# Second layer of an encoder: token rows of x through DRAM in 32x32 blocks instead of TensorE transposes

## The chip, the cores and the metric

The kernel runs on one core of a Trainium2 chip. The metric is the device time in microseconds of one execution. A core has TensorE (PE, matrix products into PSUM), VectorE (DVE), ScalarE (ACT), GpSimd (POOL) and SyncE (SP, which here only issues transfers). Transfers are carried out by 16 DMA engines that all queues share; SP, ACT and POOL issue them, and each of these queues works in its own order.

## What is computed

A two-layer encoder over 512 tokens of width 1024, in fp32: a stick-breaking attention block and an MLP, then a gated linear recurrence block and an MLP, then a last normalisation. The part that matters is the second MLP and what follows:

```
h = rms_norm(x, norm_mlp[1])
u = relu(h @ w1);  x = x + (u * u) @ w2
out = rms_norm(x, norm_final)
```

Every product is made of three fp32r products (high half times high half, low times high, high times low), so each operand is first split: ACT casts the high half (`wh`), DVE subtracts it to get the low half (`wl`).

## The kernel before

x lies with features on partitions: eight tiles `x[c]` of 128 features x 512 tokens. The MLP's hidden layer is computed in four quarters of 1024 features. The first quarter's hidden units come from `squared(c)`, c = 0 to 7 (24 matmuls each). What follows are 98 steps of 24 matmuls (2.72 us each): a "down" stage of 14 steps (indices 0 to 13) for the first quarter, then for each of three quarters an "up" stage and a "down" stage of 14 steps. In down stages the result has tokens on partitions; `y(t, h)` is the half-row h (512 features) of the token block t (128 tokens), one half of a tile c0 to c3. Products are formed by a seven-product scheme (P1 to P7), so weight blocks (`b11`, `b12`, `b22`, `b21`) are added to each other first: by DVE, or, for P7 and P4 and one P6, by a transfer on POOL that adds in place (`added`, L1096; "add" below). The result of an add is cast and split (`operand`) four steps before PE uses it.

`collect` (L1119) takes a finished product out of PSUM into `y`: where the tile is in `begun`, DVE scales it and adds it to what is there (L1125); else ACT writes it scaled (L1128) and puts it into `begun`.

Since the result must be x plus the MLP, the second layer puts x itself into `y` first. `between(c)` (L1659) is called behind each `squared(c)`; for c = 0 to 3 it transposes token block c of all eight chunks on PE into two PSUM banks, ACT copies the banks to `y` (L1670), and all eight half-rows are marked as begun. Behind c = 3, 4 and 5, `sums_of_x` (L924) overwrites x in place, chunk by chunk.

The chunks 7 of two tiles, `bh` and `bl`, hold something else early in the first down stage and are moved away by `replace` (L988, on ACT) in the steps 5, 7, 10 and 11.

The order on PE is that of the program. ACT's and DVE's steps inside the MLP are chained in program order (`Ordered`, L772). POOL's and SP's instructions are put in order at build time by a scheduler that lets ready ones pass others. The program is built with `dynamic_dma_scratch_size=1024` (L1833), the scratch for POOL's transfers. In `run`, `load(i)` (L1217) comes first in each step, then `leave(i-1)` with the collects and operands.

Of the kernel before, what the change touches and what calls it, by code (L numbers as in the profile page):

```python
# [2 lines left out]

# [8 lines left out]
F32 = mybir.dt.float32  # L12
F32R = mybir.dt.float32r
AF = mybir.ActivationFunctionType
ALU = mybir.AluOpType
PSUM = bass.MemoryType.PSUM

P = 128
S = 512
D = 1024  # L20
C = D // P
# [6 lines left out]
ASIDE, FRONT = 16, 64  # L28


START = [
# [31 lines left out]
def hybrid_encoder(  # L63
# [23 lines left out]
    nc = tc.nc  # L87
# [16 lines left out]
    def f(ap):  # L104
        return ap.bitcast(F32)
# [36 lines left out]
    bh = const.tile([P, C, S], F32R, tag="bh", name="bh")  # L142
# [164 lines left out]
    def home_tile(tag, n, name):  # L307
        return home.tile([P, S], F32, tag=tag, name=name, bufs=n)
# [482 lines left out]
    class Mlp:  # L791
# [28 lines left out]
        def __init__(self, ctx, layer):  # L820
            self.layer, self.sq, self.first = layer, Squares(), None
            self.V, self.A = Ordered(V), Ordered(A)
            self.mp = ctx.enter_context(tc.tile_pool(name=f"mlp{layer}", bufs=2))
            self.c = [
                self.mp.tile([P, 2, S], F32, tag=f"c{i}", name=f"c{i}", bufs=1) for i in range(4)
            ]
            self.begun, self.a = set(), {}
            self.turns = count(4 * layer)
            self.blocks = ExitStack()
            self.bp = self.blocks.enter_context(tc.tile_pool(name=f"blocks{layer}", bufs=2))  # L830
            self.u, self.lows, self.s3, self.slots = {}, {}, {}, None

            t = self.bp.tile([P, C // 2 * S + ASIDE], F32R, tag="s41", name="s41", bufs=1)
            self.s41 = t[:, : C // 2 * S].rearrange("p (k s) -> p k s", s=S)
# [316 lines left out]
        def run(self, first, between, end):  # L1151
# [13 lines left out]
            def place(i):  # L1165

                return (i + self.STEPS // 2) % self.STEPS
# [48 lines left out]

            def load(i):  # L1217
                q4, at = steps[i][1], place(i)

                if i == 0:  # L1220
                    self.turns = count(2)
                elif at == 0:
                    self.turns = count(4)
                    self.u.clear()
                    del self.a[1]
                elif at == 4:
                    units["down", q4] = self.from_down(q4)
                    self.load(units["down", q4], (0, "b11"), (0, "b12"), (1, "b11"))
                elif at == 11:
                    self.load(units["down", q4], (1, "b12"), (0, "b22"), (1, "b22"))  # L1230
                elif at == 14 and q4 == NQ - 1:
                    end.ready()
                elif at == 22 and q4 < NQ - 1:
                    units["up", q4 + 1] = self.from_up(q4 + 1)
                    self.load(units["up", q4 + 1], (0, "b11"), (0, "b12"), (0, "b22"), (1, "b11"))
                elif at == 25 and q4 < NQ - 1:
                    self.load(units["up", q4 + 1], (1, "b12"), (1, "b22"))
# [145 lines left out]
    with ExitStack() as mctx:  # L1383
# [29 lines left out]
        def between(c):  # L1413
            for n in {0: (0, 4), 1: (1, 5), 2: (2, 6), 3: (3,), 4: (7,)}.get(c, ()):
                nc.sync.dma_start(out=away[:, n, :], in_=x[n])
            if c == C - 1:
                soft.send(mlp.ready)
# [31 lines left out]
    with ExitStack() as rctx:  # L1449
# [44 lines left out]
        def fetch(key):  # L1494
            i = int(key[1:]) + (C if key[0] == "c" else 0)
            pool = wmore if next(fetched) % 4 == 3 else wpool
            raws[key] = pool.tile([P, C, P], F32, tag="raw", name="raw", bufs=3 if pool is wpool else 1)
            nc.sync.dma_start(out=raws[key], in_=w_ro[i] if key[0] == "o" else w_in[i])
# [157 lines left out]
    with ExitStack() as mctx:  # L1656
        mlp = Mlp(mctx, 1)

        def between(c):  # L1659

            t = c
            if t not in range(NB):
                return
            for h in range(2):
                pt = mlp.bank()
                for i in range(4):
                    PE.transpose(
                        pt[:, i * P : (i + 1) * P], x[4 * h + i][:, t * P : (t + 1) * P], ident
                    )
                A.copy(mlp.y(t, h), pt)  # L1670
                mlp.begun.add((t // 2 * 2 + h, t % 2))

        gb = []

        def factors():
            for h in range(2):
                gb.append(home_tile(*HOMES[h], "gb"))
                nc.sync.dma_start(
                    out=gb[h], in_=g_final[:, h * S : (h + 1) * S].broadcast_to([P, S])
                )  # L1680


        A.activation(mlp.c[0][:, 0, :1], eps_t, AF.Sqrt)

        free = colt[:, COLS["conv"][0] :]
        ss = free[:, : 3 * NB].rearrange("p (t i) -> p t i", i=3)
        bias = free[:, 3 * NB : 4 * NB]

        EV, EA = Ordered(V), Ordered(A)

        def square(t, h, i, cols=slice(0, S), end=False):

            junk = work.tile([P, S], F32, tag="sq", name="junk")
            EA.activation(
                junk[:, cols], mlp.y(t, h)[:, cols], AF.Square, accum_out=ss[:, t, i : i + 1]
            )
            if not end:
                EA.activation(
                    bias[:, t : t + 1], ss[:, t, i : i + 1], AF.Identity,
                    bias=bias[:, t : t + 1] if i else eps_t, scale=1.0 / D,  # L1700
                )

        def scaled(t, h, cols=slice(0, S), e=G):
            y = mlp.y(t, h)[:, cols]
            e.tensor_tensor(y, y, gb[h][:, cols], ALU.mult)

        def root(t, i):

            rt = work.tile([P, 1], F32, tag="rt", name="rt")
            EA.activation(rt, ss[:, t, i : i + 1], AF.Sqrt, bias=bias[:, t : t + 1], scale=1.0 / D)  # L1710
            EV.reciprocal(rt, rt)
            return rt

        def leaves(t, h, queue):
            queue.dma_start(out=out[t * P : (t + 1) * P, h * S : (h + 1) * S], in_=mlp.y(t, h))

        def scaled_half(t, h, rt, queue):

            y = mlp.y(t, h)
            EA.activation(y, y, AF.Copy, scale=rt)  # L1720
            leaves(t, h, queue)

        def whole_half(t, h, rt, cut=None, last=None):

            y = mlp.y(t, h)
            with tc.issue_after(last.ins) if last else nullcontext():
                EV.scalar_tensor_tensor(
                    y[:, cut:], y[:, cut:], rt, gb[h][:, cut:],
                    ALU.mult, ALU.mult,
                )  # L1730
            if cut:
                EV.tensor_scalar(y[:, :cut], y[:, :cut], rt, None, ALU.mult)
            leaves(t, h, nc.sync)

        def end(ws, xs):
            for t in range(2):
                square(t, 0, 0)
                scaled(t, 0)
                square(t, 1, 1, end=True)
                rt = root(t, 1)  # L1740
                scaled_half(t, 0, rt, nc.sync)
                whole_half(t, 1, rt, last=mlp.gained)
            for t in range(2, 4):
                square(t, 1, 0)
            scaled(2, 1)
            for g in range(2):
                mlp.times("P4", g, 0, ws[g], xs[0], False)
            mlp.collect("P4", 1, xs[1])
            for e in (EV, EA):
                e.turn(True)  # L1750
            mlp.V = EV
            mlp.collect("P4", 0, xs[0])
            square(2, 0, 1, end=True)
            halves = [slice(i * HS, (i + 1) * HS) for i in range(2)]
            ps = [mlp.bank()[:, :HS] for _ in halves]
            for i, cols in enumerate(halves):
                for g in range(2):
                    mlp.times("P4", g, 1, ws[g], ps[i], True, cols)
            mlp.collect("P4", 1, ps[0], halves[0])
            rt = root(2, 1)  # L1760
            square(3, 0, 1, halves[0])
            scaled_half(2, 1, rt, nc.sync)
            whole_half(2, 0, rt)
            mlp.collect("P4", 1, ps[1], halves[1])
            square(3, 0, 2, halves[1], end=True)
            scaled(3, 1, e=EV)
            scaled(3, 0, halves[0], e=EV)
            rt = root(3, 2)
            whole_half(3, 0, rt, HS)
            scaled_half(3, 1, rt, A)  # L1770

        end.ready = factors
        mlp.quarters(between, end)
# [69 lines left out]
```

## Time and profile before

| | us |
|---|---|
| median of 3 runs (1030.16 to 1030.9) | 1030.34 |
| the profiled execution | 1030.17 |
| its span, first to last instruction | 1028.5 |
| mean granted TensorE clock | 0.999 |
| second MLP, `squared(0)` to the end | 705 to 1028.5 |
| the 32 transposes of x, first and last start | 716.0 and 730.6 |

Times below are in us from the start of the span. PE, DVE, ACT and POOL are engines; PEld is TensorE's weight load; a name ending in q (SPq, POOLq) is an engine's queue. L1096 is a line of the kernel. A row like `b<-in_w_up` reads: written tile, read tile. `128x512` is partitions x elements. In rows of the time line the first number is the start, the second the duration (of merged rows, of all of them), and brackets hold the idle time before and what ended it.

### The profile page before, as it was taken

To read this page: it belongs to the slowest core of one execution; us is meant where nothing else is said; L and a number is where in the kernel's file an instruction comes from. 1 tells how busy PE (TensorE), PEld (TensorE's weight loads), DVE (VectorE), ACT (ScalarE), POOL (GpSimd) and SP (SyncE) were. 2 spreads that over 40 slices of the span, in tenths; PEclk is the share of its full clock that TensorE was granted. 3 is DMA by queue.
4 is the path that set the end of the run, shared out by engine and by line. 5 is a ranking of instruction groups with operands and counts; after the bars stand their busy time and mean duration, and the time that the engine had idled before them with its cause. 6 is when DMAs were issued, how large, how long until landed. Compare 5 with 4: busy or idle time off the path is not lost.

```text
span 1028.5 us, 15889 instructions
## 1 busy us (share of the span) xinstructions
PE 1020.0 (99%) x5868; PEld 891.5 (87%) x5868; DVE 859.7 (84%) x1152; ACT 715.3 (70%) x1110; POOL 172.4 (17%) x235
## 2 busy tenths in 40 slices
PE   9999999999999999999999999999999999999997
PEld 7888888888878988988988888888888988988986
DVE  7878787847897798798899889984788798898898
ACT  6777676835877774873875689964866874873865
POOL 0354344420010010010011110300010010010012
PEclk9999999999999999999999999999999999999999
DMA  7745454537646777677692574452437677677663
GB/s 233 220 123 145 109 152 103 153 110 267 152 92 185 167 161 191 165 160 194 165 228 78 149 173 128 103 204 85 101 82 190 161 164 193 166 157 196 166 122 107
DMA packets 52700, 159.41 MB, mean 155 GB/s; under 512 B 6672, under 2 KB 7952, under 8 KB 52624
## 3 DMA queue, kind: packets, MB, share of 16 engines
q1 hardware_dynamic: 41376, 119.35, 36.3%
q0 software_dynamic: 10528, 38.28, 22.2%
q8 instruction: 46, 0.75, 0.3%
q10 hardware_dynamic: 720, 0.79, 0.2%
q14 instruction: 30, 0.25, 0.1%
HBM read 137.41 MB, written 4.19 MB: 138 GB/s over the span
## 4 chain that ended last, share of the span: by engine, by line
PE 96%; DVE 2%; ACT 1%; DMA 0%; issue 0%; SPq 0%; DVEq 0%; ACTq 0%
PE ps_t L1114 15%; PE ps_acc L1019 10%; PE ps_acc L1114 8%; PE ps_z L1019 8%; PE ps_acc L239 6%; PE ps_acc L241 6%; PE ps_acc L240 6%; PE ps_o L1019 5%; PE ps_z L1114 4%; PE ps_t L239 3%; PE ps_t L240 3%; PE ps_t L241 3%; PE ps_o L239 2%; PE ps_o L240 2%; PE ps_o L241 2%; PE ps_t L626 2%
## 5 line engine op out<-in xcount | busy, mean ns | idle before, releaser
L781 ACT CAST wh<-b 128x1024 fp32r<-128x1024 f32 x168 | 174.1, 1050 | 105.8 <-DVE b L781 64.7
L781 DVE TENSOR_TENSOR wl<-b,wh 128x1024 fp32r<-128x1024 f32 x168 | 204.2, 1220 | 47.9 <-ACT wh L781 47.2
L1096 POOL DMA_DIRECT2D b<-in_w_dn x40 | 35.1, 877 | 351.7 <-DVE b L781 155.4
L239 PE MATMUL ps_acc<-xg,wh 128*128 128x512 f32 x208 | 84.8, 408 | 0.0
L241 PE MATMUL ps_acc<-xg,wh 128*128 128x512 f32 x208 | 81.6, 392 | 0.0
L240 PE MATMUL ps_acc<-xg,wl 128*128 128x512 f32 x208 | 81.5, 392 | 0.0
L1019 PE MATMUL ps_z<-xg,wh 128*128 128x256 f32 x384 | 78.6, 276 | 0.0
L234 DVE TENSOR_TENSOR wl<-raw,wh 128x512 fp32r<-128x512 f32 (+2 forms) x70 | 62.1, 912 | 14.9 <-ACT wh L232 14.8
L604 DVE TENSOR_TENSOR_SCAN scan<-keep,later 128x128 f32<-128x128 f32 (+1 forms) x64 | 58.4, 915 | 16.8 <-ACT keep L594 11.2
L781 ACT ACTIVATE u<-u 128x512 f32<-128x512 f32 x100 | 63.2, 632 | 8.7 <-DVE u L781 7.1
L232 ACT CAST wh<-raw 128x512 fp32r<-128x512 f32 (+2 forms) x70 | 50.7, 759 | 23.2 <-PE ps_acc L241 7.3
L1019 PE MATMUL ps_z<-xg,wl 128*128 128x256 f32 x240 | 66.3, 276 | 0.0
L1019 PEld LDWEIGHTS ps_z<-xg,wh 128*128 128x128 f32 x384 | 62.8, 188 | 0.0
L1019 PE MATMUL ps_acc<-xg,wh 128*128 128x256 f32 x288 | 61.4, 277 | 0.0
L608 POOL TENSOR_TENSOR w<-w,scan 128x128 f32<-128x128 f32 (+1 forms) x64 | 51.7, 808 | 56.2 <-DVE scan L604 53.3
L1096 POOL DMA_DIRECT2D b<-in_w_up x24 | 20.9, 871 | 237.1 <-DVE b L781 106.0
L781 DVE TENSOR_TENSOR b<-b,b 128x1024 f32<-128x1024 f32 x48 | 58.7, 1223 | 1.3
L781 DVE TENSOR_TENSOR u<-u 128x512 f32<-128x512 f32 (+1 forms) x92 | 54.8, 595 | 2.5 <-ACT u L781 1.1
L781 ACT CAST wh<-raw 128x1024 fp32r<-128x1024 f32 x46 | 47.9, 1044 | 7.4 <-PE ps_acc L1114 7.4
L1019 PE MATMUL ps_acc<-xg,wl 128*128 128x256 f32 x192 | 53.1, 276 | 0.0
L1019 PE MATMUL ps_acc<-low,wh 128*128 128x256 f32 x192 | 53.0, 276 | 0.0
L1114 PE MATMUL ps_t<-wh,bh 128*128 128x512 f32 x126 | 49.2, 391 | 0.0
(381 smaller groups left out, 3265.6 us busy)
## 6 DMA issues: line engine op xcount, KB each, us to landing
b<-in_w_dn SPq DMA_DIRECT2D x48, 512.0 KB, 4.5
b<-in_w_dn POOLq DMA_DIRECT2D x40, 512.0 KB, 5.5
b<-in_w_up SPq DMA_DIRECT2D x36, 512.0 KB, 4.5
b<-in_w_up POOLq DMA_DIRECT2D x24, 512.0 KB, 5.5
raw<-in_w_m SPq DMA_DIRECT2D x16, 512.0 KB, 4.1
raw<-in_w_dn SPq DMA_DIRECT2D x16, 512.0 KB, 4.6
raw<-in_w_in SPq DMA_DIRECT2D x16, 512.0 KB, 4.3
raw<-in_w_qk SPq DMA_DIRECT2D x12, 512.0 KB, 3.8
```

What stands on the lines that cost most here:

```text
L232: A.copy(wh[:, k, :], raw[:, k, :])
L234: V.tensor_tensor(wl[:, k, :], raw[:, k, :], f(wh[:, k, :]), ALU.subtract)
L239: PE.matmul(ps, wh, ah, start=start, stop=False)
L240: PE.matmul(ps, wl, ah, start=False, stop=False)
L241: PE.matmul(ps, wh, al, start=False, stop=stop)
L604: V.tensor_tensor_scan(sc[:, S - n : S][:, ::-1], keep[:, :n][:, ::-1], later[:, S - n :][:, ::-1], 1.0, ALU.mult, ALU.max,)
L608: G.tensor_tensor(wt, wt, sc[:, S - n + 1 : S + 1], ALU.mult)
L626: PE.transpose(tr[:, (qb - kb) * P : (qb - kb + 1) * P], w[pair, j, qb][:, kb * P : (kb + 1) * P], ident,)
L781: ins = getattr(self.e, name)(*args, **kwargs)
L1019: PE.matmul(ps[:, i * HS : (i + 1) * HS], m, y, start=new and i == k == n == 0, stop=i == 1 and k == C // 2 - 1 and n == 2, skip_group_che ...
L1096: G.dma_start(out=unit[b].rearrange("p j n -> p (j n)"), in_=unit["src"](to), accum_op=ALU.add)
L1114: PE.matmul(ps, m, y[:, jj, cols], start=first and n == 0, stop=last and n == 2, skip_group_check=not new,)
```

## The change

`between` no longer transposes. It stores the chunks of x to a DRAM tensor `away` (1024 x 512) on SP, in the calls c = 0 to 4. Later, a table `BY_BLOCKS` says for each half-row n = 2t + h at which step its fetch begins, how many of its four parts go per step, and at which step it is turned. `fetch(n, a)` reads 32 tokens of 512 features into 32 partitions of the chunk 7 of `bh` (n even) or `bl` (n odd), as 32 x 16 runs of 32 elements, so that each 32x32 block lies transposed; it is issued on POOL. `turned(n)` turns the blocks by one DVE transpose into the tile `blocks` (a single buffer), and a transfer on POOL adds that to `y`. Nothing is marked as begun any more, so the first collect of each half-row is ACT's.

```diff
+BLOCK = 32
+BY_BLOCKS = (
+    (12, 2, 17), (14, 1, 21), (18, 1, 25), (28, 1, 44), (32, 1, 47), (45, 1, 52), (56, 1, 72), (60, 1, 75),
+)
...
             def load(i):
                 q4, at = steps[i][1], place(i)
+                for do in self.aside.get(i, ()):
+                    do()
...
+        dram = mctx.enter_context(tc.tile_pool(name="dram1", bufs=1, space=bass.MemoryType.DRAM))
+        away = dram.tile([D, S], F32, tag="away", name="away")
+        blocks = {}
+
         def between(c):
-
-            t = c
-            if t not in range(NB):
-                return
-            for h in range(2):
-                pt = mlp.bank()
-                for i in range(4):
-                    PE.transpose(
-                        pt[:, i * P : (i + 1) * P], x[4 * h + i][:, t * P : (t + 1) * P], ident
-                    )
-                A.copy(mlp.y(t, h), pt)
-                mlp.begun.add((t // 2 * 2 + h, t % 2))
+            for n in {0: (0, 4), 1: (1, 5), 2: (2, 6), 3: (3,), 4: (7,)}.get(c, ()):
+                nc.sync.dma_start(out=away[n * P : (n + 1) * P, :], in_=x[n])
+
+        def fetch(n, a):
+
+            if a == 0:
+                blocks[n] = f((bh, bl)[n % 2][:, C - 1, :])
+            t, h = divmod(n, 2)
+            rows = slice(a * BLOCK, (a + 1) * BLOCK)
+            at = t * P + a * BLOCK
+            G.dma_start(
+                out=blocks[n][rows, :].rearrange("k (j i) -> k j i", i=BLOCK),
+                in_=away[h * S : (h + 1) * S, at : at + BLOCK].rearrange(
+                    "(j k) i -> k j i", k=BLOCK
+                ),
+            )
+
+        def turned(n):
+
+            to = home_tile(*HOMES[C - 1], "blocks")
+            mlp.V.transpose(out=to, in_=blocks.pop(n))
+            G.dma_start(out=mlp.y(*divmod(n, 2)), in_=to, accum_op=ALU.add)
+
+        for n, (at, by, done) in enumerate(BY_BLOCKS):
+            for a in range(P // BLOCK):
+                mlp.aside.setdefault(at + a // by, []).append(partial(fetch, n, a))
+            mlp.aside.setdefault(done, []).append(partial(turned, n))
```

On PE, behind `squared(1)`, before (L1667 is the transpose, L239 to L241 the three products of a slab):

```order
L241 MATMUL ps_acc<-xg,wh 128x512
L1667 MATMUL ps_z<-ident,x 128x128 x8
L1667 MATMUL ps_o<-ident,x 128x128 x8
L239 MATMUL ps_t<-xg,wh 128x512
L240 MATMUL ps_t<-xg,wl 128x512
```

and now (five lines of the program further down):

```order
L246 MATMUL ps_acc<-xg,wh 128x512
L244 MATMUL ps_z<-xg,wh 128x512
L245 MATMUL ps_z<-xg,wl 128x512
```

The next slab's matmuls follow directly, in another bank.

On POOL, from the last adds of the first down stage (in_w_dn) to those of the first up stage (in_w_up; b12 is P7's add, b11 P4's), before:

```order
L1096 DMA b11_7428<-in_w_dn 128x1024
L1096 DMA b11_7432<-in_w_dn 128x1024
L1096 DMA b12_7983<-in_w_up 128x1024
L1096 DMA b11_7981<-in_w_up 128x1024
L1096 DMA b12_8045<-in_w_up 128x1024
L1096 DMA b11_7987<-in_w_up 128x1024
```

and now (L1101 is the add, L1681 the fetch, L1692 the adding transfer):

```order
L1101 DMA b11_7431<-in_w_dn 128x1024
L1101 DMA b11_7435<-in_w_dn 128x1024
L1681 DMA bh_78<-away_7364 32x16x32 x4
L1681 DMA bl_79<-away_7364 32x16x32 x4
L1101 DMA b12_7946<-in_w_up 128x1024
L1101 DMA b11_7944<-in_w_up 128x1024
L1692 DMA c0_7354<-blocks_8172 128x512
L1681 DMA bh_78<-away_7364 32x16x32 x4
L1101 DMA b12_8008<-in_w_up 128x1024
L1101 DMA b11_7950<-in_w_up 128x1024
```

The eight fetches of half-rows 0 and 1 stand ahead of the up stage's first add, and those of half-row 2, behind the first adding transfer, ahead of its third.

Also on POOL, from there to the second down stage, now:

```order
L1692 DMA c1_7355<-blocks_8315 128x512
L1681 DMA bl_79<-away_7364 32x16x32 x4
L1692 DMA c0_7354<-blocks_8452 128x512
L1681 DMA bh_78<-away_7364 32x16x32 x4
L1101 DMA b12_8208<-in_w_dn 128x1024
L1101 DMA b11_8206<-in_w_dn 128x1024
L1101 DMA b12_8455<-in_w_dn 128x1024
```

The fetches of half-rows 3 and 4, which the table puts at the steps 28 to 35, stand ahead of all adds of that stage. The order is the same further on: half-row 5 is ahead of the third add of the next up stage, half-row 6 ahead of the fourth.

More of the change, by code (lines that the diff above doesn't have):

```diff
@@ L1 @@
 from contextlib import ExitStack, nullcontext
+from functools import partial
 from itertools import chain, count, islice
@@ L826, in __init__ @@
             ]
-            self.begun, self.a = set(), {}
+            self.begun, self.a, self.aside = set(), {}, {}
             self.turns = count(4 * layer)
```

## The prediction

> **What bounds the kernel now.** I read the page first, then PE's waits, then the stages of the second layer's MLP.
>
> ```profile
> PE 1020.0 (99%) x5868; PEld 891.5 (87%) x5868; DVE 859.7 (84%) x1152; ACT 715.3 (70%) x1110; POOL 172.4 (17%) x235
> PE 96%; DVE 2%; ACT 1%; DMA 0%; issue 0%; SPq 0%; DVEq 0%; ACTq 0%
> PE ps_acc L1114 <- DVE wl L781: 0.5, 1, 0.5
> 770.00:805.00 35.00, 35.00 (x212) 31.07 (x211) 28.24 (x31) 23.48 (x32) 2.62 (x3) 1.00 0.74 201
> 805.00:840.00 35.00, 35.00 (x267) 33.13 (x266) 31.34 (x35) 29.51 (x40) 4.39 (x5) 1.00 0.68 151
> ```
>
> The first two rows are busy time by engine and the chain of waits by engine: TensorE (PE) is the chain for 96% of the span. The third is PE's only wait inside an MLP, 0.5 us. The last two are stages (stage, PE, weight loads, DVE, ACT, POOL, clock, share of the DMA engines, GB/s): PE never rests, the clock is full, POOL is nearly idle. So every microsecond of PE work taken out comes off the end, as long as all operands still arrive in time.
>
> **What is removed.** 32 transposes on PE and their eight evictions on ACT. In the time line PE's starts tell the price, not its durations, since matmuls overlap:
>
> ```profile
> 716.26 1.04 PE L1667 MATMUL ps_z<-ident,x 128*128 128x128 f32 x8
> 717.93 0.48 PE L239 MATMUL ps_t<-xg,wh 128*128 128x512 f32 x1
> 718.24 0.40 PE L240 MATMUL ps_t<-xg,wl 128*128 128x512 f32 x1
> 718.47 0.39 PE L241 MATMUL ps_t<-xg,wh 128*128 128x512 f32 x1
> 723.47 0.60 PE L1667 MATMUL ps_t<-ident,x 128*128 128x128 f32 x4
> 724.27 0.48 PE L239 MATMUL ps_acc<-xg,wh 128*128 128x512 f32 x1
> 729.81 1.04 PE L1667 MATMUL ps_z<-ident,x 128*128 128x128 f32 x8
> 730.61 0.48 PE L239 MATMUL ps_o<-xg,wh 128*128 128x512 f32 x1
> ```
>
> The 16 of between(0) and between(1) hold PE from 716.26 to 717.93, 1.67 us; those of between(2) 0.80; those of between(3) 0.80. The matmul behind each group starts its successor after 0.31 us instead of 0.23 (717.93, 718.24, 718.47), 0.08 three times. Together 3.5 us. I take all of it; the least would be 2.7, if DVE, which the one wait above shows at its limit, moved forward only by the first two groups (1.67 + 0.80 + 2 x 0.08).
>
> The row of one transpose by itself says 272 ns, and the Trainium skill ("TensorE: Matmul & The Clock Gate", Part 4: PE-mode transpose) gives about 275 ns for one inside a kernel. By that price the 32 would be worth 8.8 us; here the starts show some 0.1 us each, so the trace agrees with the duration but not with it as a cost.
>
> **What is moved between ACT and DVE.** ACT loses eight copies and gains eight first collects; DVE loses eight collects and gains eight block transposes.
>
> ```profile
> L1128 ACT ACTIVATE c<-ps_t,rr 128x512 f32<-128x512 f32 x6 | 4.0, 687 | 4.7 <-PE ps_t L1114 4.7
> L1670 ACT COPY c<-ps_z 128x512 f32<-128x512 f32 x4 | 2.2, 592 | 0.0
> 765.80 0.74 DVE L781 SCALAR_TENSOR_TENSOR c<-ps_t,rr,c 128x512 f32<-128x512 f32 x1
> ```
>
> The first layer already collects on ACT (L1128, 0.69 us each), and PE's waits show no stall there. No row has a DVE block transpose; a 128x512 collect is 0.74 and a transpose with half as many inputs may be a little less or, at worst, twice. Both exchanges I take at 0: the freed copies and collects cover them, and in 805 to 840 DVE has 3.7 us free. Without that cover eight times 0.7, or 5.6 us, would be at stake.
>
> **What is added on SP.** Eight stores of x (256 KB) between slab loads. SP's last slab loads, ACT's first overwriting of x, and the times to landing (least, median, most) of the first layer's transfers of x to and from DRAM:
>
> ```profile
> 689.93 28.99 SPq L226 DMA_DIRECT2D raw<-in_w_m  x6
> 732.45 1.33 ACT L781 ACTIVATE x<-x,colt 128x512 f32<-128x512 f32 x2
> DMA to landing us min/median/max: 2.1/5.9/9.8
> ```
>
> SP has issued its last slab by 718.9, the stores stand ahead of the last two, and x is first overwritten at 732.45, more than 9.8 us later. So they are done in time: 0. Were they late, ACT's in-place scaling of x would wait, up to those 9.8 us.
>
> **What is added on POOL.** 32 fetches (64 KB each, in 512 pieces of 128 bytes) and eight adding transfers. POOL works in order, and its queue already holds the adds of weight blocks, whose results ACT and DVE must turn into operands before PE comes to them. An adding transfer itself costs POOL what an add does, 0.88, and has time: half-row 2 goes out at step 25 and its tile is next collected in at step 31, 16 us later, against a landing after 5.5. In the new order eight fetches stand ahead of the first up quarter's first add (b12, for P7). The rows of that place (the last is the time from issue to landing of the adds):
>
> ```profile
> 776.37 0.40 ACT L781 CAST xg<-bh 128x256 fp32r<-128x256 f32 x1
> 788.28 0.87 POOL L1096 DMA_DIRECT2D b<-in_w_up  x1 [16.92 <-DVE b L781]
> 798.21 1.05 ACT L781 CAST wh<-b 128x1024 fp32r<-128x1024 f32 x1
> 799.15 1.05 ACT L781 CAST wh<-raw 128x1024 fp32r<-128x1024 f32 x1
> 799.29 1.23 DVE L781 TENSOR_TENSOR wl<-b,wh 128x1024 fp32r<-128x1024 f32 x1 [3.09 <-ACT wh L781]
> 800.43 1.22 DVE L781 TENSOR_TENSOR wl<-raw,wh 128x1024 fp32r<-128x1024 f32 x1
> 803.08 0.28 PE L1019 MATMUL ps_acc<-xg,wl 128*128 128x256 f32 x1
> DMA to landing us min/median/max: 5.2/5.5/7.5
> ```
>
> The fetch of half-row 0 may start when the chunk of bh is free, 776.8. The add is issued at 788.28 and lands 5.5 us later; the cast takes 0.94 to the next start, DVE's low half 1.14 (799.29 to 800.43), and PE wants the low half at 803.08. So the add may land as late as 801.0 and be issued as late as 795.5. Between 776.8 and 795.5 lie 18.7 us. With a time C from one fetch's issue to the next, the eight need 7C + 0.87, so **PE is untouched up to C = 2.55 us**, and beyond it is late by 7 (C - 2.55).
>
> What C is, no row shows. The rows nearest to it:
>
> ```profile
> L1466 POOL DMA_DIRECT2D graw<-in_w_gate x2: 564/582/599, 564.2 to 566.5; - x2
> DMA to landing us min/median/max: 2.9/3.3/3.7
> kh<-xh SPq DMA_DIRECT2D x28, 128.0 KB, 2.6
> 828.97 0.87 POOL L1096 DMA_DIRECT2D b<-in_w_dn  x1 [14.95 <-DVE b L781]
> 831.32 0.87 POOL L1096 DMA_DIRECT2D b<-in_w_dn  x1 [1.48 <-DVE wl L781]
> ```
>
> POOL's one plain load from DRAM (graw, 128 rows of 2 KB) holds it 0.58 us and lands after 3.3. If POOL only writes descriptors and goes on, C lies between 0.58 (the same) and 2.33 (four times as many pieces, four times the time): under 2.55 at both ends. If a fetch can't be issued before the one ahead of it has landed, C is the landing time: 2.6 (the small transfers of kh) to 3.7 (graw at its slowest). The trace speaks weakly for the second: POOL never has more than a few transfers of 128 rows in flight (831.32 was issued 2.4 us after the add before it, within its 5.5 us), while two fetches are 1024 pieces. I take the second and C = 3.0, between the transfer nearest in size (2.6) and the one nearest in kind (3.3).
>
> The kernel reserves 1024 bytes of scratch for such transfers. The Trainium skill ("DMA: Bandwidth & Descriptors", SWDGE vs HWDGE vs iDMA) says that GpSimd writes 16-byte descriptors into rings in SBUF that take one place per partition in two groups of 16; by that, an estimate, a ring has 64 places for each transfer engine, and a fetch wants 32 and one for its end, so that two don't fit. No row of this trace can show it.
>
> **The sum.** Four places on POOL have fetches in front of an add. The first is the one above; when PE wants the low half at the other three:
>
> ```profile
> 822.15 0.28 PE L1019 MATMUL ps_z<-xg,wl 128*128 128x256 f32 x1
> 844.21 0.39 PE L1114 MATMUL ps_t<-wl,bh 128*128 128x512 f32 x1
> 904.03 0.28 PE L1019 MATMUL ps_z<-xg,wl 128*128 128x256 f32 x1
> ```
>
> Each is worked out like the first, in the old clock, later ones moved by what went before. (1) 776.8 + 21.87 = 798.7, landed 804.2, low half 806.3 against 803.1: 3.2 late. (2) The first adding transfer waits for the block transpose behind two more low halves (808.1); 0.88, then four fetches, and the add issues at 818.9, low half at 826.5 against 822.15 + 3.2: 1.2 more. (3) Fetches 3 and 4 (half-rows) stand ahead of the first down adds: issue 844.2, low half 851.8 against 844.2 + 4.4: 3.2 more. (4) Fetches 5 and 6 are ahead of the last add of the next up quarter: issue 906.4, low half 914.0 against 904.0 + 7.6: 2.4 more.
>
> Stalls 10.0, gain 3.5: +6.5 us. The profiled execution took 1030.17 us (span 1028.5 and 1.7 around it), the median of the runs is 1030.34, 0.2 apart; so I add to the median: **1036.8 us**. With C at 2.6 the same four places give 2 us of stall (net -1.5), at 3.7 some 27 (net +24).
>
> **The rivals.** *POOL runs on* (C under 2.55): no stall, 1030.3 - 3.5 = 1026.8. For it speaks that descriptor writing alone stays under the limit at both bounds; against it that 2.33 leaves almost nothing, and that nothing in the trace shows 1024 pieces in flight. *The pieces clog the transfer engines*: in 770 to 805 these are busy 0.74 already, and the 16384 pieces fall into the 130 us from there. Per engine that is 1024; if one took 0.05 us, 51 us in 130, the share would pass 1, and bulk loads would arrive late too; it decides from about 0.03 us a piece. Time with C at 3.7 or more: 1054 and up. Against it: 64 KB is an eighth of an add. *The gain is eaten elsewhere* (ACT's in-order queue behind a late add, 2 to 5 us of stalls, or C between 2.55 and 2.85): 1029 to 1032.
>
> **How the numbers follow.** One fetch at a time 0.46, POOL runs on 0.36, clogged engines 0.08, eaten 0.10. Less than 0.2% (2.1 us) either way can't be told from no change. The forecast's own range is 1030 to 1054; to hold 8 in 10 it must reach down to the rival without stalls: 1026 to 1054. Faster 0.36 (POOL runs on), the same 0.10 (eaten), slower 0.54.
>
> **What would show it.** In the changed profile: PE without L1667 and its first down step 3.5 us earlier; fetches on POOL that start 2.6 to 3.7 us apart, each ended by the landing of the one before; PE's waits with "wl" released late at about 803, 822, 844 and 904 and ACT's casts waiting for adds. The forecast is wrong if fetches follow each other in under 2.5 us and PE shows no new wait, or if late SP loads, not adds, are what ACT waits for.

## The result and the profile after

The changed kernel takes 1076.91 us (median of 6 runs, 1073.32 to 1077.9); the kernel before, beside it, 1030.57 (1029.59 to 1031.12). The ratio is 1.0443, 95% interval 1.0428 to 1.0459: 46 us slower, where 6.5 were forecast and 1054 was the end of the range.

The page of the changed kernel, busy time by engine, the granted clock in 40 slices, and the chain of waits by engine:

```profile
PE 1024.2 (95%) x5836; PEld 895.4 (83%) x5836; DVE 859.8 (80%) x1152; ACT 716.1 (67%) x1110; POOL 197.7 (18%) x275
PEclk9999999999999999999999999999998879979999
PE 82%; issue 8%; DVE 3%; DMA 3%; POOL 2%; ACT 2%; DVEq 0%; SPq 0%; POOLq 0%; ACTq 0%
```

PE was 96% of the chain and is now 82%; 8% is "issue", time in which an engine waits for nothing that the profile shows. PE's waits from 780 us on (total, times, longest):

```profile
PE ps_z L1024 <- ACT u L786: 19.2, 2, 12.0
PE ps_t L1119 <- DVE c L786: 12.8, 1, 12.8
PE ps_acc L1024 <- ACT u L786: 9.3, 1, 9.3
```

Four stalls make 41.3 us. PE waits for PSUM banks that ACT (`u`) or DVE (`c`) has not emptied. The stages (PE, weight loads, DVE, ACT, POOL, clock, share of the DMA engines, GB/s):

```profile
770.00:805.00 35.00, 29.36 (x178) 26.00 (x176) 17.25 (x18) 16.75 (x25) 7.17 (x10) 0.97 0.53 154
805.00:840.00 35.00, 24.08 (x180) 23.88 (x181) 23.26 (x24) 21.53 (x27) 7.06 (x9) 0.79 0.64 150
```

PE, DVE and ACT are idle more (POOL, which issues the fetches, is busier), and the DMA engines too: 0.53 and 0.64, before 0.74 and 0.68. Nothing is saturated; something is late. POOL's time line at the first place (start, duration, and in brackets the idle time ahead and what ended it), and then, from the view of the fetches' line, how long and how often POOL sat idle before one with "issue" as the reason, and the times to landing:

```profile
774.62 0.72 POOL L1681 DMA_DIRECT2D bh<-away  x1 [7.62 <-ACT xg L786]
779.97 0.68 POOL L1681 DMA_DIRECT2D bh<-away  x1 [4.63 <-issue]
785.48 0.66 POOL L1681 DMA_DIRECT2D bh<-away  x1 [4.83 <-issue]
788.19 0.65 POOL L1681 DMA_DIRECT2D bh<-away  x1 [2.05 <-issue]
...
799.71 0.65 POOL L1681 DMA_DIRECT2D bl<-away  x1 [1.97 <-issue]
800.36 0.98 POOL L1101 DMA_DIRECT2D b<-in_w_up  x1
810.50 0.88 POOL L1692 DMA_DIRECT2D c<-blocks  x1 [7.37 <-DVE blocks L786]
811.13 0.94 POOL L1681 DMA_DIRECT2D bh<-away  x1
818.31 0.70 POOL L1681 DMA_DIRECT2D bh<-away  x1 [6.24 <-issue]
```

```profile
  issue: 88.6, 29
DMA to landing us min/median/max: 2.3/2.4/6.8
```

A fetch holds POOL for 0.66 us, and ahead of 29 of the 32 POOL stands still for 88.6 us, 3.06 each (one more stop, of 2.0 us, is put down to ACT). Each of these 30 fetches starts 0.30 to 0.38 us behind a landing: 26 behind that of the fetch ahead, four (837.26, 908.01, 926.08, 944.57) behind that of an add. How long a landing takes differs. Here are the first three fetches, each from its issue to its landing, in the columns of the stages above:

```profile
774.62:779.60 4.98, 4.98 (x23) 4.12 (x23) 4.64 (x6) 4.38 (x6) 0.72 (x1) 1.00 0.79 243
779.97:785.17 5.20, 5.20 (x25) 4.31 (x24) 5.03 (x7) 2.94 (x5) 0.68 (x1) 1.00 0.70 243
785.48:787.88 2.40, 2.40 (x12) 1.97 (x12) 2.07 (x2) 0.69 (x1) 0.66 (x1) 1.00 0.13 27
```

With the DMA engines 0.79 and 0.70 busy a fetch lands after 5.0 and 5.2 us, with 0.13 after 2.4. Of all 32, 19 land after 2.3 to 2.5 us, 18 of them at a share of 0.08 to 0.33, and 13 after 3.2 to 6.8, 12 of them at 0.45 to 1.01.

The add issues at 800.36. What that does, on ACT's time line and on PE's:

```profile
793.95 0.59 ACT L786 COPY u<-ps_acc 128x512 f32<-128x512 f32 x1 [2.13 <-PE ps_acc L1024]
806.14 1.04 ACT L786 CAST wh<-b 128x1024 fp32r<-128x1024 f32 x1 [11.60 <-DMA b<-in_w_up]
807.09 1.04 ACT L786 CAST wh<-raw 128x1024 fp32r<-128x1024 f32 x1
808.04 0.58 ACT L786 COPY u<-ps_acc 128x512 f32<-128x512 f32 x1
```

```profile
799.08 0.28 PE L1024 MATMUL ps_acc<-low,wh 128*128 128x256 f32 x1
808.67 0.58 PE L1024 MATMUL ps_acc<-xg,wh 128*128 128x256 f32 x1 [9.31 <-ACT u L786]
809.04 0.41 PE L1024 MATMUL ps_acc<-xg,wl 128*128 128x256 f32 x1
...
813.08 0.28 PE L1024 MATMUL ps_acc<-low,wh 128*128 128x256 f32 x1
813.19 0.28 PE L1024 MATMUL ps_acc<-xg,wh 128*128 128x256 f32 x1
```

ACT stands at the cast of the late block for 11.60 us, and the copy that frees PE's bank is two casts behind it in ACT's order. PE starts again as the copy ends. From there to 813.0 its matmuls start 0.21 us apart, afterwards 0.11: half rate for 4.4 us, with a granted clock of 0.50. The same follows the other three stalls (to 840.3, 877.9 and 953.0), so some 17 us pass at about half rate, about 8 lost. That explains the sum: 41.3 + 8, less the 2.65 that the change saves (e4 below), is 46.7, and 46.3 was measured.

### The profile page after: what moved, and what is told of

Same layout as the page of the kernel before. It is cut to its first block, busy times and chain, and to the rows that moved or that the text cites. A ratio compares the mean times of both kernels' runs of the same rounds, so it can differ in the third digit from the quotient of the medians.

```text
span 1075.1 us, 15899 instructions
## 1 busy us (share of the span) xinstructions
PE 1024.2 (95%) x5836; PEld 895.4 (83%) x5836; DVE 859.8 (80%) x1152; ACT 716.1 (67%) x1110; POOL 197.7 (18%) x275
## 4 chain that ended last, share of the span: by engine, by line
PE 82%; issue 8%; DVE 3%; DMA 3%; POOL 2%; ACT 2%; DVEq 0%; SPq 0%; POOLq 0%; ACTq 0%
PE ps_t L1119 15%; PE ps_acc L1119 7%; PE ps_acc L1024 6%; PE ps_z L1024 6%; PE ps_acc L244 5%; PE ps_acc L246 5%; PE ps_acc L245 5%; PE ps_z L1119 3%; PE ps_o L1024 3%; PE ps_t L244 2%; PE ps_t L245 2%; PE ps_t L246 2%; PE ps_o L244 2%; PE ps_o L245 2%; PE ps_o L246 2%
## 5 line engine op out<-in xcount | busy, mean ns | idle before, releaser
L1024 PE MATMUL ps_z<-xg,wh 128*128 128x256 f32 x384 | 82.0, 285 | 19.2 <-ACT u L786 19.2
L1101 POOL DMA_DIRECT2D b<-in_w_dn x40 | 35.3, 889 | 312.3 <-DVE b L786 119.1
L1024 PEld LDWEIGHTS ps_z<-xg,wh 128*128 128x128 f32 x384 | 65.4, 195 | 19.6 <-ACT u L786 19.6
L244 PE MATMUL ps_acc<-xg,wh 128*128 128x512 f32 x200 | 81.7, 409 | 0.0
L246 PE MATMUL ps_acc<-xg,wh 128*128 128x512 f32 x200 | 78.4, 392 | 0.0
L245 PE MATMUL ps_acc<-xg,wl 128*128 128x512 f32 x200 | 78.4, 392 | 0.0
L239 DVE TENSOR_TENSOR wl<-raw,wh 128x512 fp32r<-128x512 f32 (+2 forms) x70 | 61.6, 905 | 17.4 <-ACT wh L237 17.2
L1024 PEld LDWEIGHTS ps_acc<-xg,wh 128*128 128x128 f32 x288 | 48.9, 191 | 9.7 <-ACT u L786 9.5
L1101 POOL DMA_DIRECT2D b<-in_w_up x24 | 21.3, 886 | 181.1 <-DVE b L786 80.0
```

The source lines that it names most:

```text
L239: V.tensor_tensor(wl[:, k, :], raw[:, k, :], f(wh[:, k, :]), ALU.subtract)
L244: PE.matmul(ps, wh, ah, start=start, stop=False)
L245: PE.matmul(ps, wl, ah, start=False, stop=False)
L246: PE.matmul(ps, wh, al, start=False, stop=stop)
L1024: PE.matmul(ps[:, i * HS : (i + 1) * HS], m, y, start=new and i == k == n == 0, stop=i == 1 and k == C // 2 - 1 and n == 2, skip_group_che ...
L1101: G.dma_start(out=unit[b].rearrange("p j n -> p (j n)"), in_=unit["src"](to), accum_op=ALU.add)
```

## The experiments

Theory **R** (room): POOL's scratch holds the descriptors of one fetch; POOL stands still until there is room, and the adds behind the fetches are late. **P** (pieces): the 128-byte pieces occupy the transfer engines. **T**: the block transposes on DVE or ACT's first collects are late. In the table the waits are the sum of PE's waits from 780 us on, and the rest is the profiled span less 1026.5 (the span of e4) less the waits; in the runs with a stall of 2.2 us or more most of it is half-rate time. Both are of the profiled execution, which in e7 is the slowest of its ten (1033.63).

| run | us | ratio to before (95%) | PE's waits | rest |
|---|---|---|---|---|
| the changed kernel | 1076.91 | 1.0443 (1.0428 to 1.0459) | 41.3 | 7.3 |
| e4 without fetches | 1027.95 | 0.9976 (0.9966 to 0.9986) | 0 | 0 |
| e1 1152 bytes | 1047.05 | 1.0159 (1.0141 to 1.0178) | 14.4 | 5.2 |
| e5 1088 bytes | 1046.88 | 1.0169 (1.0152 to 1.0186) | 12.2 | 5.6 |
| e2 half fetches | 1053.73 | 1.0220 (1.0201 to 1.0240) | 20.7 | 5.7 |
| e9 whole rows | 1029.64 | 0.9993 (0.9983 to 1.0002) | 1.0 | 1.2 |
| e3 program order | 1045.32 | 1.0146 (1.0129 to 1.0163) | 13.4 | 3.2 |
| e7 order, 1152 bytes | 1031.51 | 1.0013 (1.0003 to 1.0022) | 2.6 | 2.7 |
| e6 fetches on SP | 1029.78 | 0.9997 (0.9987 to 1.0006) | 1.2 | 1.2 |
| e8 on SP, other table | 1028.89 | 0.9986 (0.9977 to 0.9995) | 0 | 1.3 |

### What the change saves: e4

```diff
-        for n, (at, by, done) in enumerate(BY_BLOCKS):
...
-            mlp.aside.setdefault(done, []).append(partial(turned, n))
```

> The changed kernel without its fetches, block transposes and adding transfers; it leaves out adding x to the result (the stores of x stay, and all first collects are ACT's). It measures what the change saves on PE. R: 1030.3 less 3.5 is 1026.8, with 1025.5 to 1028.5 as the range, no stall on PE over 0.5 us. T in the form that ACT's first collects or SP's stores cost time: 1035 or more.

1027.95 us, 2.65 less than the 1030.6 beside it (1.4 to 3.5 by the interval), and no wait of PE from 780 us on. So the stores on SP and the first collects on ACT cost nothing that shows. T in that form falls. The saving is a little under the 3.5 of the sum.

### More room: e1 and e5

```diff
-    nc = _bacc.Bacc("TRN2", target_bir_lowering=False, num_devices=1, dynamic_dma_scratch_size=1024)
+    nc = _bacc.Bacc("TRN2", target_bir_lowering=False, num_devices=1, dynamic_dma_scratch_size=1152)
```

> The changed kernel with 1152 bytes of scratch for POOL's transfers in place of 1024, nothing else. Theory R (the scratch holds the descriptors of one fetch, so POOL stands still at each fetch until the one before it is done; the adds behind come late, ACT stands in order at their casts, PE runs out of banks): two fetches now fit, those of a run go out 1.3 to 1.8 us apart in the mean in place of 2.7 to 5.5, the first up quarter's first add is issued by 791 in place of 800.4, three or all of the four stalls (41 us) go and the slow clock behind them with them: 1027 to 1040 us. Rival P (512 pieces of 128 bytes keep the transfer engines 2.7 us busy whoever issues them): same pace, 1073 to 1078. Rival T (the block transposes on DVE or the first collects on ACT make the bank evictions late, not the adds): 1073 to 1078.

> The changed kernel with 1088 bytes of scratch, 64 more than it has. Theory R with its arithmetic: a descriptor of 16 bytes for each of 32 pieces per transfer engine and one for the end make 33, so two fetches need 66 places of 16 bytes, 1056 bytes. 1024 holds one, 1088 holds two: the fetches go out in pairs as with 1152 bytes, and the time is that of e1_two_fit, 1043 to 1051 us. If room helps by degrees (more of it, a little less waiting), this step of a half of that to 1152 gives about half of e1's gain: 1060 to 1066. If the threshold lies elsewhere: 1073 to 1078 as with 1024.

POOL's time line with 1088 bytes, at the same place:

```profile
775.41 1.39 POOL L1681 DMA_DIRECT2D bh<-away  x2 [7.62 <-ACT xg L786]
781.16 1.30 POOL L1681 DMA_DIRECT2D bh<-away  x2 [4.36 <-issue]
786.53 1.30 POOL L1681 DMA_DIRECT2D bl<-away  x2 [4.07 <-PE ps_t L1119]
789.26 1.30 POOL L1681 DMA_DIRECT2D bl<-away  x2 [1.43 <-issue]
792.03 1.83 POOL L1101 DMA_DIRECT2D b<-in_w_up  x2 [1.48 <-issue]
```

The order on POOL is the same to the row, but the fetches now go out in pairs, and the add issues 8 us earlier. 64 bytes more gave 30 us, and the next 64 none (1046.88 and 1047.05): a threshold, not a slope. P and T would have left the time at 1073 to 1078. R's size was missed, though: 1047, not 1027 to 1040. A fetch lands after 4.1 us in the median where it was 2.4 (least, median, most); below that row is the stretch from the issue to the landing of the fetch at 786.53:

```profile
DMA to landing us min/median/max: 2.3/4.1/6.6
786.53:788.95 2.42, 2.42 (x13) 1.99 (x12) 1.88 (x2) 0.69 (x1) 1.29 (x2) 1.00 0.26 54
```

That isn't the second fetch's doing: this one had another beside it and landed after 2.4 us, with the DMA engines 0.26 busy. The pairs at 775.41 and 781.16 landed after 4.9 to 5.5, with 0.90 and 0.69. So a fetch took 2.1 us in the mean from 775.4 to 792.0, not 1.3 to 1.8, and later places, where a fetch follows an adding transfer in flight, still stall.

### Smaller transfers: e2

```diff
+            for j in range(2):
+                cols, first = slice(j * HS, (j + 1) * HS), h * S + j * HS
-            G.dma_start(
+                G.dma_start(
...
```

> The changed kernel with each fetch cut into two of 256 pieces, scratch 1024 as it was; the same pieces, twice the transfers. R: three halves fit into the scratch at once, so a half waits only for the third one back: 0.7 to 1.0 us a half, 1.4 to 2.0 a whole fetch, first up add issued by 793: 1028 to 1045 us. P: the pieces are the same, so the pace of a whole fetch stays 2.7 us or more: 1070 to 1085. T: 1073 to 1085. If what a fetch costs is a fixed landing time per transfer and POOL waits for each one whatever its size, it is 64 waits of some 2.3 us in place of 32 and slower than now: 1100 and more.

POOL's time line at the first place (the second stop is put down to a transfer of weights, but it ends 0.33 us behind the landing of the first half):

```profile
771.23 1.84 POOL L1683 DMA_DIRECT2D bh<-away  x3 [3.90 <-ACT xg L786]
775.38 1.81 POOL L1683 DMA_DIRECT2D bh<-away  x3 [2.31 <-DMA b<-in_w_up]
780.04 1.24 POOL L1683 DMA_DIRECT2D bh<-away  x2 [2.86 <-issue]
```

Three halves go out back to back, then POOL stands. So POOL doesn't wait for each transfer: the rival of 1100 us falls, and P's unchanged pace too (23 us gained). R's direction holds; its size (1028 to 1045) was again missed, by 9 us, for the same reason: the nine halves issued up to 781.6 land after 2.9 to 5.1 us (the DMA engines are 0.91 busy from 771.2 to 785.2), the next seven after 2.0 to 2.2 (0.20).

### The same bytes in fewer pieces: e9

```diff
             G.dma_start(
-                out=blocks[n][rows, :].rearrange("k (j i) -> k j i", i=BLOCK),
-                in_=away[h * S : (h + 1) * S, at : at + BLOCK].rearrange(
-                    "(j k) i -> k j i", k=BLOCK
-                ),
+                out=blocks[n][rows, :], in_=away[n * P + a * BLOCK : n * P + (a + 1) * BLOCK, :]
             )
```

> The changed kernel with the same 32 fetches on POOL, at the same places of its queue and of the same 64 KB, but each of 32 whole rows of 2 KB in place of 512 pieces of 128 bytes; scratch 1024. It leaves out the transposition (what is added to the result is not x by token rows). R, by pieces: what fills the scratch is the number of pieces, so with a sixteenth of them nothing stands still: fetches 0.5 to 1.0 us apart, the order of POOL's queue alone costs at most 8 times 0.7 at the first place, under the 18.7 us that it has: 1027 to 1031 us. If POOL takes on a fixed number of such transfers at a time, whatever their pieces (the landing of one being 2.3 at best): still 2 to 3 us apart, 1055 or more. If the place in the order is what costs: 1073 to 1078.

POOL's time line at the first place (merged rows, durations summed):

```profile
775.79 2.04 POOL L1681 DMA_DIRECT2D bh<-away  x4 [7.48 <-ACT xg L786]
783.67 1.96 POOL L1681 DMA_DIRECT2D bl<-away  x4 [5.84 <-ACT xg L786]
785.74 0.92 POOL L1101 DMA_DIRECT2D b<-in_w_up  x1
```

This is the cleanest of them: same scratch, same places in POOL's queue, same bytes, a sixteenth of the pieces. Four fetches go out back to back, "issue" is gone from their waits, the add issues at 785.74 in place of 800.36, and the time is 1029.64. So the place in POOL's order costs nothing by itself, and what fills the scratch is pieces. T falls with it: the block transposes and ACT's first collects are all there. The transfers' own landing (least, median, most) is no shorter:

```profile
DMA to landing us min/median/max: 2.4/5.3/7.4
```

A late landing is therefore not the pieces' doing (the first one takes 4.99 us, with the DMA engines 0.83 busy), and no fetch waits for it here.

### Other order: e3 and e7

```diff
-            self.V, self.A = Ordered(V), Ordered(A)
+            self.V, self.A, self.G = Ordered(V), Ordered(A), Ordered(G)
+            self.G.turn(layer == 1)
...
-                G.dma_start(
+                self.G.dma_start(
```

(the same for the two transfers of `fetch` and `turned`); e7 adds the 1152 bytes.

> The changed kernel with POOL's adds, fetches and adding transfers of the second layer chained in program order, so that no fetch passes an add that comes earlier in the program; scratch 1024. R: fetches still stand still 2.7 to 5.5 us apart, but at most four stand between two adds (as a rule one or two), which is 11 to 15 us at the worst place: the stalls shrink to 0 to 10 us, 1028 to 1042 us. P: the same pieces in the engines, other transfers as slow as now: over 1055. T: 1073 to 1078.

> e3's program order on POOL together with e1's 1152 bytes of scratch. R: e3 lost its 6.7 us on PE behind a run of five fetches and an add at 805 to 822 us, each standing still 2 to 7 us; with room for two, these waits halve: 1029 to 1038 us. If room and order are the same remedy (whichever comes first takes all that can be had), 1043 to 1047.

Where e3 still loses 6.7 us on PE, at 818 to 825, POOL's time line reads:

```profile
813.12 0.66 POOL L786 DMA_DIRECT2D bh<-away  x1 [2.35 <-issue]
813.77 0.97 POOL L786 DMA_DIRECT2D b<-in_w_up  x1
815.76 0.68 POOL L786 DMA_DIRECT2D bh<-away  x1 [1.01 <-issue]
821.73 0.90 POOL L786 DMA_DIRECT2D b<-in_w_up  x1 [5.29 <-issue]
```

Here the add itself stands 5.29 us behind the fetch and the add ahead of it, and starts 0.26 us behind the landing of that add (7.69 us), with the fetch still in flight: room again. e3 came out 3 us above its range. With room for two, one stall of 2.2 us and waits of 0.2 are left and the time is 1031.51, inside the range, some 14 and 16 us below the two remedies alone. Order decides how many fetches an add must sit behind, room how long each takes.

### Another issuer: e6, and e8

```diff
-            G.dma_start(
+            nc.sync.dma_start(
                 out=blocks[n][rows, :].rearrange("k (j i) -> k j i", i=BLOCK),
```

> The changed kernel with its 32 fetches issued by SP in place of POOL (same pieces, same DRAM, scratch 1024; POOL keeps the adds and the adding transfers). R: POOL has no fetch to stand still at, every add goes out when its block is free, so the four stalls and the slow clock behind them go: 1026 to 1032 us, near the 1027.95 of e4 without the addition of x. Rival P (the pieces occupy the transfer engines): adds and slabs land later than in e4, 1040 or more. Rival S (the wait only moves: SP stands at a fetch until chunk 7 of bh or bl is free, and weight blocks behind it come late): 1035 to 1060, with PE or ACT waiting for transfers of SP.

SP's time line at the four fetches of half-row 1 (merged, their durations summed):

```profile
783.70 2.04 SPq L1681 DMA_DIRECT2D bl<-away  x4
```

SP issues these 512-piece transfers some 0.5 us apart, with no stop between them (over all 32, one holds SP for 0.48 us in the median and 1.21 at most). 1029.78 us: P (1040 or more) and S (1035 or more) fall. PE's waits from 780 us on, two for `sl` and one for an eviction:

```profile
PE ps_z L1024 <- ACT u L786: 0.7, 1, 0.7
PE ps_t L1119 <- DVE sl L786: 0.5, 2, 0.3
```

e8 moves the block transposes to the first third of each up stage, and with them the fetches of the half-rows 3, 4, 5 and 7:

```diff
-    (12, 2, 17), (14, 1, 21), (18, 1, 25), (28, 1, 44), (32, 1, 47), (45, 1, 52), (56, 1, 72), (60, 1, 75),
+    (12, 2, 16), (14, 1, 19), (18, 1, 44), (21, 1, 47), (45, 1, 50), (48, 1, 72), (56, 1, 75), (73, 1, 78),
```

> e6 (fetches on SP) with another table: the block transposes at the steps 16, 19, 44, 47, 50, 72, 75 and 78, the first third of each up stage, in place of 17, 21, 25, 44, 47, 52, 72 and 75. In e6 PE lost 0.83 us at 820 (ACT's eviction late) and about 1.5 us in small waits at 834 to 839 and 912 to 916, when DVE makes the low halves sl with a block transpose of 0.70 us ahead of it. If the transposes at the steps 21, 25 and 52 are the cause, these waits go: 1028.0 to 1029.2 us, 0.1 to 0.25% under the kernel before, no wait of PE for sl. If the waits come from the transfers (fetches between weight blocks on SP): 1029.5 to 1031 as e6.

Both waits are gone, and 1028.89 us is 0.14% under the kernel before (0.05% to 0.23%): the change does pay, once its fetches are off POOL, by about 1.5 of the 2.65 us that e4 shows. That e8 is faster than e6 rests on the trace; the two intervals overlap. And since fetches moved too, it isn't shown that the block transposes alone made e6's waits.

## Why the prediction was wrong

**Direction and mechanism held.** The forecast's own case was the one that happened: one fetch at a time, POOL in order, adds late, four stalls in the four places named (before the up stage's first adds, behind half-row 2, at the first down adds, behind half-rows 5 and 6). The forecast ended on the right side, but its chance (0.54 slower) and its range gave the rival "POOL runs on" too much: its case was descriptor writing at 0.58 to 2.33 us, and at 0.66 us it was true of the writing alone. e9 shows that rival's world: with pieces that fit, POOL does run on. One sign was named wrong: PE's waits were to be for the low half (`wl`), and they are for banks that ACT or DVE has not emptied.

**The term that failed is the price C of a fetch**, 3.0 us with 3.7 as its upper end, one value for every fetch. It came from the landing times of other transfers. In the trace it is 0.66 + 3.06, or 3.72, in the mean of the 29 that stood, but not evenly. Where the DMA engines have little else to do, a landing takes 2.3 to 2.5 us and fetches follow each other every 2.7, less than was forecast. The single gaps of 5.35, 5.51 and 7.18 are landings of 5.0, 5.2 and 6.8 us of the fetch ahead, with the engines 0.79, 0.70 and 0.73 busy. So what the sum lacked, by the shares beside the landings, is that a fetch takes its turn with the weight loads and adding transfers that run beside it (the prediction's own row for the transfers of x, 2.1/5.9/9.8, has such a spread). No run varied that traffic alone. By the prediction's own formula 3.7 gives 27 us of stalls in place of 10.

The side of the forecast was in part luck: between its 2 us of stalls for C = 2.6 and its 10 for 3.0, the 2.7 of a fetch beside idle engines would have made some 4 (an estimate), about the gain of 3.5.

The first place can be followed to the end. One row of the kernel before is wanted, PE's first start on the bank of that stall:

```profile
802.96 0.28 PE L1019 MATMUL ps_acc<-xg,wh 128*128 128x256 f32 x1
```

3.2 us were forecast, 9.31 came. Seven gaps of 3.58 (774.62 to 799.71) in place of 3.0 are 4.1. PE came to the place 3.6 earlier (799.36, the end of its last matmul, against 802.96), but the first fetch only 2.2 (774.62 against 776.8): the gain itself took 1.4 of the slack, which the sum kept in the old clock. The cast of the added block began 5.8 us behind the add's issue, not 5.5, and PE waited for the copy's end at 808.62, behind both casts, not for the low half (0.3 each). 3.2 + 4.1 + 1.4 + 0.6 is 9.3. For the other three I did not split the 14 us between 27 and 41.3 by place; late starts (each follows a late adding transfer) and gaps of 4 to 7 us stand in POOL's time line there.

**A term was missing:** the half rate behind each long stall, about 8 us. The sum took a stall to cost its own length.

**Other terms.** The gain of 3.5 measured 2.65 (e4, 1.4 to 3.5); the least that the prediction named was 2.7. The exchange between ACT and DVE at 0 was nearly so: e6 to e8 is about 1 us, which the trace puts at transposes ahead of low halves that PE is waiting for (not shown alone, since fetches moved too). The stores on SP at 0 held (e4). The rival "pieces clog the transfer engines" is excluded by e6 (same pieces, no loss) and by the DMA share, which fell; its time, 1054 and up, would have fitted. "Eaten elsewhere", with 1029 to 1032, describes e6, e7 and e9 but not this kernel.

The Trainium skill ("DMA: Bandwidth & Descriptors", Terms) speaks of 16-byte descriptors that are written to rings in SBUF; the estimate from it, 33 places of a 64-place ring for each fetch, asks for 1056 bytes for two. The trace agrees: 1024 bytes hold one fetch or three halves (e2), 1088 hold two (e5). Where between 1024 and 1088 the threshold lies, no run shows.

**What stays open.** That an add's descriptors fill the scratch as a fetch's do was not tried alone; it is read from the fetches that start right behind an add's landing, and from the add of e3 that does. Nor was the wait for the eviction separated from that for the operand by an experiment, only by the rows above. And that the traffic of weight loads and adding transfers makes a fetch land late is read from the DMA share beside each landing, not from a run of its own.

## What to carry to other kernels

A transfer of many small pieces on POOL is to be counted in pieces against the scratch for descriptors, not in bytes: if two don't fit, everything behind on POOL waits for a whole landing (here 2.4 us beside idle transfer engines, 3.2 to 6.8 beside other transfers), and if POOL also carries loads that PE needs, that is the price. Put such transfers on a queue whose issuer doesn't stand still, or keep them behind the loads, or give them room; each of these alone took back some 30 us or more (47, 32 and 30). And price a stall with what follows it: the time that TensorE runs at half rate afterwards, and the queue that is blocked in order behind the late operand.

## What was not expected of the hardware

How short a pause brings the half rate. In e7 a pause of 2.20 us was enough, and the half rate set in 0.8 us after PE had started again (PE's time line):

```profile
822.85 0.39 PE L1025 MATMUL ps_z<-xg,wh 128*128 128x256 f32 x1 [2.20 <-ACT u L786]
823.07 0.28 PE L1025 MATMUL ps_z<-xg,wl 128*128 128x256 f32 x1
823.19 0.28 PE L1025 MATMUL ps_z<-low,wh 128*128 128x256 f32 x1
...
823.65 0.41 PE L1025 MATMUL ps_z<-xg,wh 128*128 128x256 f32 x1
823.85 0.41 PE L1025 MATMUL ps_z<-xg,wl 128*128 128x256 f32 x1
...
827.05 0.29 PE L1025 MATMUL ps_z<-xg,wl 128*128 128x256 f32 x1
827.18 0.28 PE L1025 MATMUL ps_z<-low,wh 128*128 128x256 f32 x1
```

It cost another 1.5 us (3.4 us at half rate). In e5 a pause of 2.33 us, up to 848.75, did the same: the granted clock is 0.50 from 850.2 to 853.6. In e3 a pause of 2.11 us cost nothing: the matmuls behind it start 0.23 us apart at once and stay so. What decides between them is not shown. Behind the long stalls of the changed kernel the clock falls in the pause itself: PE stops at 799.36, and the granted clock is 1.00 up to 802.8 and 0.50 from there to 813.0. Its stretches at 0.50 last 10.24, 6.83, 13.65 and 13.66 us, those behind the short pauses of e5 and e7 3.4: multiples of 3.41. The Trainium skill ("TensorE: Matmul & The Clock Gate", Why this matters for your kernels) advises to keep idle gaps under about 3 us; here 2.20 was already too long in e7, and 2.33 in e5.
